# S5 input side: the powers of B one f tile ahead of their transposes, in four fixed slots

## The chip, the cores and the metric

The kernel runs on one core of one Trainium2 chip. The metric is the device time of one execution in microseconds. In the profile PE is TensorE (PEld its weight loads), DVE is VectorE, ACT is ScalarE, POOL is GpSimd, and SP is the engine whose queue issues most of the DMA loads.

## The reference

Two layers act on x of 256 positions by 2048 channels: gated linear attention first, then S5, a complex-diagonal state-space layer. Each has a residual and a layer norm. Of the S5 layer (inner width 4096 = 256 groups of 16 channels, 64 complex states a group) this is the part that matters here:

```
u, z = split(u_in @ w_in)                      # 2 x 4096 columns
lb   = exp(a * dt)                             # lambda, a group's 64 states
bb   = coef * b                                # 64 x 16 a group
x[t] = lb * x[t-1] + bb @ u[t]                 # complex, per group
y[t] = Re(c @ x[t]) + d * u[t]
y    = gelu(y); y = y * sigmoid(y @ w_glu + b_glu); out = (y * silu(z)) @ w_out
```

The kernel does the recurrence in chunks of 8 positions. For that it needs B multiplied by the powers 0 to 7 of lambda (the states' input over a chunk, and the kernel inside a chunk), and a scan over 32 chunks.

## The kernel before, in words

All large products are made from fp32 weights split into a high part (an ACT cast, `hi...`, line 145) and a low part (a DVE subtraction, `lo...`, line 146), and three matmuls on these parts stand for one product. A step of the weight loop is called a block here: one 128 x 1024 piece of weights, its split, and 24 matmuls of 128x128 by 128x256 (lines 180 to 182).

The stage around the change makes u ("su"): eight column groups g = 0 to 7, each of eight blocks kp = 0 to 7. Behind each block, the loop takes steps from a list `bq` as `b_pace` allows (`bstep`), and small steps from another list (`pump`), among them from the end of g = 4 on the 30 scan steps of the first half (`scan`, lines 1187 to 1189). The list `bq` goes through the 256 groups in 32 tiles f of 8 groups, two tiles f = 2p and 2p + 1 to a pair p = 0 to 15:

- `bload(p)` loads B and the powers of lambda of a pair (tile `rb`, two buffers, lines 1056 and 1058, issued on the SP queue), `kload` loads C (`rc`, line 1066).
- `b_pow(f)` makes B times the powers: an ACT copy (line 1091) for power 0 and three DVE instructions of 128x896 for powers 1 to 7 (two products, lines 1096 and 1097, the second into the tile `pt` with one buffer; a subtraction, line 1098). The result is half of the pair's tile `wu[p]`, which the trace calls wb.
- `b_tr(f)` transposes it: twice four PE transposes into a PSUM bank (line 1107, pswb), each four followed by an ACT copy (line 1108) into half of the pair's tile `wb[p]`, which the trace calls wbt.
- `s_mm(p)` multiplies u by it, and C by the powers: 128 small matmuls (lines 1128 and 1133), then two DVE transposes into the states sx (line 1139) and two ACT copies (line 1141).
- `k_out(p)` transposes the chunk's kernel (line 1149), copies it (1152), adds d on POOL (1155, 1158) and stores it with two DMAs of the POOL queue (1161) to dk.

At the end of each g, `s_in(g)` copies the four PSUM banks to the tile vv (ACT, line 1114), stores it (du, line 1115) and loads it back in another order into half of `Ut[g // 2]` (line 1116), both on the POOL queue. s_mm(p) reads `Ut[p // 4]`.

The tiles u1 (four), Ut (four), wu and wb share one pool, `s8`, of twelve slots. Before the change each pair makes a new wu and a new wb tile.

The program's order is not the order on the engines: the tile framework hands out the slots and orders each engine's instructions ahead of time, by its own estimate of when each can start; among those that can start, the one that stands first in the program goes first. On the chip each engine then runs its own list in order.

The last blocks of bq run under g = 0 of the next stage ("sz", the z half of w_in). The steps of bq before the change, in order: f = 0, f = 1; then for each p from 1: s_mm(p - 1), f = 2p, f = 2p + 1, and from p = 2 on k_out(p - 2). With `b_pace` the two first steps run behind kp = 3 and kp = 7 of g = 0, and from kp = 4 of g = 1 on one step runs behind each block.

Of the kernel before, what the change touches and what calls it, by code (L numbers as in the profile page):

```python
# [15 lines left out]
P = 128  # L16
# [17 lines left out]
def trunk(ctx, tc, x, c, ln_g, ln_b, ada_w, ada_b, gla_w_in, gla_gate_w2, gla_gate_b, gla_norm_g,  # L34
# [3 lines left out]
    V, S, PE = nc.vector, nc.scalar, nc.tensor  # L38
# [35 lines left out]
    def s8t(name, shape, dt=F32):  # L74
        return s8.tile([P] + shape, dt, tag="s8", name=name)
# [4 lines left out]
    def psx(name):  # L80
        return ax.tile([P, 512], F32, tag="ax", name=name)

    ident = cp.tile([P, P], F32, name="ident")
# [50 lines left out]
    def wload(src, k0, c0, name, last=False):  # L134
        w = wp.tile([P, 1024], F32, tag="w", name="w" + name) if last else ring.take("w" + name)
        dma(w.rearrange("p (k c) -> p k c", k=2),
            src[k0 * P:(k0 + 2) * P, c0:c0 + 512].rearrange("(k p) c -> p k c", p=P))
        return w
# [3 lines left out]
    def split(w, name):  # L142
        hi = his.take("hi" + name)
        lo = los.take("lo" + name)
        S.copy(hi, w)  # L145
        last_lo[0] = V.tensor_tensor(lo, w, hi.bitcast(F32), op=ALU.subtract).ins  # L146
        return hi.rearrange("p (k c) -> p k c", k=2), lo.rearrange("p (k c) -> p k c", k=2)
# [75 lines left out]
    ps = psx("psc")  # L223
# [225 lines left out]
    ps = psx("psv2")  # L449
# [395 lines left out]
    for h in range(4):  # L845
        ps = psx(f"psst{h}")
        for cc, (r, a, b) in enumerate(((0, 0, 256), (64, 64, 256), (0, 256, 384), (64, 320, 384))):
            for t in range(2):
                PE.matmul(ps[r:r + 64, a:b], lhsT=kt[:, 2 * h + t, cc * 64:cc * 64 + 64], rhs=qs[cc][:, 2 * h + t, :],
                          start=(t == 0), stop=(t == 1))  # L850
# [62 lines left out]
    for g in range(8):  # L913
# [3 lines left out]
        for kp in range(8):  # L917
            for _ in range(-(-len(hq) // (8 * (2 - g % 2) - kp))):
                hq.pop(0)()
            w = split(wload(win, 2 * kp, 6144 + g * 512, f"z{g}{kp}"), f"z{g}{kp}")  # L920
            st_step(banks, u0, w, kp, 15)
            pump(Z_RATE)
        for f in range(4):
            i = (g * 4 + f) % 8
# [103 lines left out]
    for k in range(16):  # L1028
        ps = psx(f"psn{k}")
# [18 lines left out]
    def Uv(f):  # L1048
        return Ut[f // 8][:, (f % 8) // 4, :, f % 4, :]
# [3 lines left out]
    def bload(f2):  # L1053

        a = tp.tile([P, 2, 384], F32, tag="rb", name=f"rb{f2}", bufs=2)
        dma(a[:, :, 0:256], rec[:, 2 * f2:2 * f2 + 2, 128:384])
        for h in range(2):
            dma(a[64 * h:64 * h + 64, :, 256:384], rec[64 - 64 * h:128 - 64 * h, 2 * f2:2 * f2 + 2, 256:384])
        rb[f2] = a
# [3 lines left out]
    def kload(f2):  # L1063

        a = rc[f2] = tp.tile([P, 2, 144], F32, tag="rc", name=f"rc{f2}", bufs=2)
        dma(a, rec[:, 2 * f2:2 * f2 + 2, 0:144])

    wb = {}

    def powmul(o, t, a0, a1, l):  # L1070

        n = o.shape[2]
        bc = lambda z: z.rearrange("p (g i) -> p g i", g=8).unsqueeze(2).to_broadcast([P, 8, n, 16])
        lv = l.rearrange("p (r g n) -> p r g n", r=2, g=8)
        lq = lambda r: lv[:, r, :, :n].unsqueeze(3).to_broadcast([P, 8, n, 16])
        V.tensor_tensor(o, bc(a0), lq(0), op=ALU.mult)
        V.tensor_tensor(t, bc(a1), lq(1), op=ALU.mult)

    wu, kts, Upair = {}, {}, {}

    def b_pow(f):
        p = f // 2
        if f % 2 == 0:

            if p < 15:
                bload(p + 1)

            wu[p] = s8t(f"wb{p}", [2, 8, 16, 8])
        a = rb[p][:, f % 2]
        w = wu[p][:, f % 2]  # L1090
        S.copy(w[:, :, :, 0], a[:, 128:256].rearrange("p (g i) -> p g i", g=8))
        t_ = tp.tile([P, 8, 16, 7], F32, tag="pt", name=f"pt{f}", bufs=1)
        bc = lambda z: z.rearrange("p (g i) -> p g i", g=8).unsqueeze(3).to_broadcast([P, 8, 16, 7])
        lv = a[:, 0:128].rearrange("p (r g n) -> p r g n", r=2, g=8)
        lq = lambda r: lv[:, r, :, :7].unsqueeze(2).to_broadcast([P, 8, 16, 7])
        V.tensor_tensor(w[:, :, :, 1:8], bc(a[:, 128:256]), lq(0), op=ALU.mult)
        V.tensor_tensor(t_, bc(a[:, 256:384]), lq(1), op=ALU.mult)
        V.tensor_tensor(w[:, :, :, 1:8], w[:, :, :, 1:8], t_, op=ALU.subtract)

    def b_tr(f):  # L1100
        p = f // 2
        if f % 2 == 0:
            wb[p] = s8t(f"wbt{p}", [2, 8, 128])
        for h in range(2):
            ps = psx(f"pswb{f}{h}")
            for g in range(4):
                PE.transpose(ps[:, g * P:(g + 1) * P], wu[p][:, f % 2, 4 * h + g].rearrange("p i s -> p (i s)"), ident)
            S.copy(wb[p][:, f % 2, 4 * h:4 * h + 4, :], ps.rearrange("p (g r) -> p g r", g=4))

    def s_in(g, banks):  # L1110

# [7 lines left out]
    def s_mm(p):  # L1119
        pss = [psx(f"pss{2 * p + i}") for i in range(2)]  # L1120
        for i in range(2):
            f = 2 * p + i
            U = Uv(f)
            cc = rc[p][:, i]

            for b in range(2):
                for q in range(4):
                    PE.matmul(pss[i][32 * q:32 * q + 32, b * P:(b + 1) * P], lhsT=U[:, 2 * q + b],
                              rhs=wb[p][:, i, 2 * q + b, :], start=True, stop=True)
            for b in range(2):  # L1130
                for q in range(4):
                    g = 2 * q + b
                    PE.matmul(pss[i][32 * q:32 * q + 32, T + b * P:T + (b + 1) * P], lhsT=cc[:, g * 16:g * 16 + 32],
                              rhs=wu[p][:, i, g].rearrange("p i n -> p (i n)"), start=True, stop=True)
        kt_ = tp.tile([P, 2, 2, P], F32, tag="kt", name=f"kT{p}", bufs=1)
        for i in range(2):
            f = 2 * p + i
            n = 2 * (f % 16)
            V.transpose(sx[:, f // 16, 1:33, :, n:n + 2].rearrange("p c r b -> p b r c"),
                        pss[i][:, :T].rearrange("p (b r l) -> p b r l", b=2, r=4))  # L1140
            S.copy(kt_[:, i].rearrange("p b (n i) -> p b n i", n=8), pss[i][:, T:].rearrange("p (b i n) -> p b n i", b=2, i=16))
        kts[p] = kt_

    def k_out(p):
        kt_ = kts[p]
        pk_ = psx(f"psk{p}")
        for i in range(2):
            for b in range(2):
                PE.transpose(pk_[:, (2 * i + b) * P:(2 * i + b + 1) * P], kt_[:, i, b], ident)
        ks = tp.tile([P, 2, P], F32, tag="ks", name=f"ks{p}", bufs=1)  # L1150
        for i in range(2):
            S.copy(ks[:, i].rearrange("p (q b i) -> p q b i", q=4, b=2),
                   pk_[:, i * T:(i + 1) * T].rearrange("p (b q i) -> p q b i", b=2, q=4)[:, :, :, :16])
        dm = tp.tile([16, 16, 16], F32, tag="dm", name=f"dm{p}", bufs=1)
        nc.gpsimd.tensor_tensor(dm, ident[:16, :16].unsqueeze(1).to_broadcast([16, 16, 16]),
                                dT[:, 16 * p:16 * p + 16].unsqueeze(2).to_broadcast([16, 16, 16]), op=ALU.mult)
        kv = ks[:16].rearrange("p f c -> p (f c)")
        nc.gpsimd.tensor_tensor(kv, kv, dm.rearrange("p g i -> p (g i)"), op=ALU.add)
        for i in range(2):
            f = 2 * p + i  # L1160
            wdma(dk[16 * f:16 * f + 16, 896:1920].rearrange("i (n c) -> n i c", n=8), ks[:, i])


    bq = []
    for p in range(18):
        if 1 <= p < 17:
            bq.append(lambda p=p: s_mm(p - 1))
        for f in (2 * p, 2 * p + 1):
            if f < 32:
                bq.append(lambda f=f: (kload(f // 2) if f % 2 else None, b_pow(f), b_tr(f)))  # L1170
        if p >= 2:
            bq.append(lambda p=p: k_out(p - 2))

    bload(0)
    b_pace = [0.0]
# [15 lines left out]
    for g in range(8):  # L1191
        banks = [psm(f"su{g}{f}") for f in range(4)]
        for kp in range(8):

            with tc.issue_after(normed1) if (g, kp) == (0, 2) else nullcontext():
                w = split(wload(sw, 2 * kp, g * 512, f"su{g}{kp}"), f"su{g}{kp}")
            st_step(banks, u1, w, kp, 15)

            if (g, kp) == (0, 3):
                mid = more(1, 1)  # L1200
            if (g, kp) == (1, 0):
                b_pace[0] = -4.0
            b_pace[0] += 1.0 if g else 0.25
            n = max(0, int(b_pace[0]))
            bstep(n)
            b_pace[0] -= n
            pump(SCAN_RATE)
        s_in(g, banks)
        if g == 4:
            bg.extend([lambda cidx=cidx: scan(cidx, 0) for cidx in range(1, 31)])  # L1210
# [61 lines left out]
    for g in range(8):  # L1272
        banks = [psm(f"sz{g}{f}") for f in range(4)]
        for kp in range(8):
            w = split(wload(sw, 2 * kp, E + g * 512, f"sz{g}{kp}"), f"sz{g}{kp}")
# [4 lines left out]
        for f in range(4):  # L1280
            i = (g * 4 + f) % 8
# [42 lines left out]
    for g in range(8):  # L1324
        banks = [psm(f"gl{g}{f}") for f in range(4)]
        for kp in range(16):
            w = split(wload(s5_w_glu[0], 2 * kp, g * 512, f"gl{g}{kp}"), f"gl{g}{kp}")
# [14 lines left out]
        for f in range(4):  # L1342
            i = g * 4 + f
# [78 lines left out]
    ps = psx("psnb")  # L1422
# [33 lines left out]
```

## Time and profile before

| | |
|---|---|
| time, median of 3 runs | 1836.67 us (1836.52 to 1839.31) |
| time of the profiled execution | 1838.83 us |
| its span, first to last instruction | 1837.1 us |
| mean granted TensorE clock | 0.991 |
| PE busy in the span | 1781.8 us, 97% |
| DVE busy | 1410.3 us, 77% |
| ACT busy | 895.4 us, 49% |
| POOL busy | 88.0 us, 5% |
| HBM read | 437.01 MB |

The stage su lies at about 762 to 1019 us of the span. In the rows of the profile, times are microseconds from the span's start. A row of the timeline has the start, the duration, the engine, the line of the kernel, the operation, what it writes from what it reads, the number of instructions merged, and in brackets the idle time before it and what ended that. A row of the windows has for each engine its busy time and, in brackets, the number of instructions, then the granted clock of PE, the DMA engines' busy share and GB/s.

### The profile page before, as it was taken

To read this page: it belongs to the slowest core of one execution; us is meant where nothing else is said; L and a number is where in the kernel's file an instruction comes from. 1 tells how busy PE (TensorE), PEld (TensorE's weight loads), DVE (VectorE), ACT (ScalarE), POOL (GpSimd) and SP (SyncE) were. 2 spreads that over 40 slices of the span, in tenths; PEclk is the share of its full clock that TensorE was granted. 3 is DMA by queue.
4 is the path that set the end of the run, shared out by engine and by line. 5 is a ranking of instruction groups with operands and counts; after the bars stand their busy time and mean duration, and the time that the engine had idled before them with its cause. 6 is when DMAs were issued, how large, how long until landed. Compare 5 with 4: busy or idle time off the path is not lost.

```text
span 1837.1 us, 33664 instructions
## 1 busy us (share of the span) xinstructions
PE 1781.8 (97%) x13491; PEld 1574.5 (86%) x13491; DVE 1410.3 (77%) x1880; ACT 895.4 (49%) x1266; POOL 88.0 (5%) x94
## 2 busy tenths in 40 slices
PE   7999999999999999999999999999999999999997
PEld 5776897899999888899998999988888888888886
DVE  4887757879999988687699689888577775557556
ACT  4433557556556333654554535545445444444332
POOL 0000000000000000002233300000000000000000
PEclk9999999999999999999999999999999999999998
DMA  9997975879889998486665577999688886668653
GB/s 343 387 342 247 294 247 162 284 258 325 290 289 321 335 356 289 160 264 204 194 202 168 170 213 217 234 246 233 218 278 269 275 271 208 187 192 324 194 185 92
DMA packets 246101, 457.86 MB, mean 249 GB/s; under 512 B 19828, under 2 KB 49198, under 8 KB 244662
## 3 DMA queue, kind: packets, MB, share of 16 engines
q1 hardware_dynamic: 239320, 436.02, 74.1%
q0 software_dynamic: 5856, 18.63, 3.1%
q8 instruction: 106, 1.74, 0.4%
q10 hardware_dynamic: 768, 1.05, 0.2%
q14 instruction: 51, 0.42, 0.1%
HBM read 437.01 MB, written 18.61 MB: 248 GB/s over the span
## 4 chain that ended last, share of the span: by engine, by line
PE 78%; DVE 11%; DMA 4%; issue 3%; ACT 2%; POOL 0%; SPq 0%; DVEq 0%; ACTq 0%; POOLq 0%
PE gl L192 13%; PE gl L193 7%; PE op L168 6%; PE op L169 6%; PE op L167 6%; PE z L182 3%; PE z L181 3%; PE z L180 3%; PE v L168 3%; PE v L169 2%; PE v L167 2%; PE su L180 2%; PE su L181 2%; PE su L182 2%; PE sz L180 2%
## 5 line engine op out<-in xcount | busy, mean ns | idle before, releaser
L146 DVE TENSOR_TENSOR logl<-wgl,higl 128x1024 fp32r<-128x1024 f32 x128 | 156.7, 1224 | 116.0 <-ACT higl L145 111.2
L145 ACT CAST higl<-wgl 128x1024 fp32r<-128x1024 f32 x128 | 134.4, 1051 | 172.4 <-PE gl L192 167.5
L192 PE MATMUL gl<-yp,higl 128*128 128x512 f32 x512 | 179.4, 395 | 0.1
L192 PE MATMUL gl<-yb,higl 128*128 128x512 f32 x512 | 179.1, 395 | 0.0
L145 ACT CAST hio<-wo 128x1024 fp32r<-128x1024 f32 x95 | 100.2, 1055 | 152.8 <-PE op L169 131.9
L146 DVE TENSOR_TENSOR loo<-wo,hio 128x1024 fp32r<-128x1024 f32 x95 | 116.5, 1228 | 66.8 <-ACT hio L145 64.8
L317 DVE SCALAR_TENSOR_TENSOR acc<-wa,cs,acc 128x512 f32<-128x512 f32 x217 | 162.7, 750 | 2.9 <-DMA wa<-in_ada_w 0.2
L180 PE MATMUL sz<-u1h,hisz 128*128 128x256 f32 x512 | 150.4, 294 | 2.3 <-ACT zs L1284 2.3
L180 PE MATMUL su<-u1h,hisu 128*128 128x256 f32 x512 | 151.3, 297 | 0.0
L180 PE MATMUL z<-u0h,hiz 128*128 128x256 f32 x512 | 148.7, 290 | 0.0
L182 PE MATMUL sz<-u1h,losz 128*128 128x256 f32 x512 | 144.5, 283 | 2.1 <-DVE losz L146 2.1
L182 PE MATMUL su<-u1h,losu 128*128 128x256 f32 x512 | 145.8, 285 | 0.0
L181 PE MATMUL su<-u1l,hisu 128*128 128x256 f32 x512 | 145.6, 284 | 0.0
L182 PE MATMUL z<-u0h,loz 128*128 128x256 f32 x512 | 144.9, 283 | 0.6 <-DVE loz L146 0.6
L181 PE MATMUL z<-u0l,hiz 128*128 128x256 f32 x512 | 144.7, 283 | 0.0
L181 PE MATMUL sz<-u1l,hisz 128*128 128x256 f32 x512 | 144.7, 283 | 0.0
L193 PE MATMUL gl<-yb,logl 128*128 128x256 f32 x512 | 143.0, 279 | 0.0
L193 PE MATMUL gl<-yp,logl 128*128 128x256 f32 x512 | 142.3, 279 | 0.0
L145 ACT CAST hisz<-wsz 128x1024 fp32r<-128x1024 f32 x64 | 67.0, 1049 | 113.6 <-PE sz L181 57.4
L192 PEld LDWEIGHTS gl<-yp,higl 128*128 128x128 f32 x512 | 95.9, 188 | 22.9 <-issue 0.6
L192 PEld LDWEIGHTS gl<-yb,higl 128*128 128x128 f32 x512 | 96.0, 188 | 22.6
L145 ACT CAST hiz<-wz 128x1024 fp32r<-128x1024 f32 x64 | 67.2, 1051 | 88.2 <-PE z L181 80.8
(322 smaller groups left out, 5000.8 us busy)
## 6 DMA issues: line engine op xcount, KB each, us to landing
wgl<-in_s_w_glu SPq DMA_DIRECT2D x128, 512.0 KB, 4.8
wa<-in_ada_w SPq DMA_DIRECT2D x116, 512.0 KB, 5.2
wv<-in_gla_w_in SPq DMA_DIRECT2D x64, 512.0 KB, 6.5
wz<-in_gla_w_in SPq DMA_DIRECT2D x64, 512.0 KB, 5.4
wsu<-in_s_w_in SPq DMA_DIRECT2D x64, 512.0 KB, 4.5
wsz<-in_s_w_in SPq DMA_DIRECT2D x64, 512.0 KB, 5.7
wo<-in_s_w_out SPq DMA_DIRECT2D x64, 512.0 KB, 4.7
a<-in_ada_w SPq DMA_DIRECT2D x31, 1024.0 KB, 10.7
```

Source lines behind the costliest of these rows:

```text
L145: S.copy(hi, w)
L146: last_lo[0] = V.tensor_tensor(lo, w, hi.bitcast(F32), op=ALU.subtract).ins
L167: PE.matmul(banks[tt], lhsT=uh, rhs=hi[:, kk, :], start=(k == first), stop=False)
L168: PE.matmul(banks[tt], lhsT=uh, rhs=lo[:, kk, :], start=False, stop=False)
L169: last_mm[0] = PE.matmul(banks[tt], lhsT=ul, rhs=hi[:, kk, :], start=False, stop=(k == last)).ins
L180: PE.matmul(o, lhsT=wh, rhs=u.hi(k), start=(k == first), stop=False)
L181: PE.matmul(o, lhsT=wh, rhs=u.lo(k), start=False, stop=False)
L182: last_mm[0] = PE.matmul(o, lhsT=wl, rhs=u.hi(k), start=False, stop=(k == last)).ins
L192: PE.matmul(banks[f], lhsT=hi[:, kk, fs], rhs=u.both(k), start=(k == 0), stop=False)
L193: PE.matmul(banks[f][:, :T], lhsT=lo[:, kk, fs], rhs=u.hi(k), start=False, stop=(k == last))
L317: V.scalar_tensor_tensor(acc[0], w[:, kk, :], cs[:, k:k + 1], acc[0], op0=ALU.mult, op1=ALU.add)
```

## The change

`wu` and `wb` become four tiles that are made once, two of each, and used in turn by pairs (index p % 2). `b_pow(f + 1)` now stands ahead of `b_tr(f)` in the step of f, with `b_pow(0)` as a first step of its own; `bload(p + 1)`, which `b_pow(2p)` issues, moves with it. The counter at the start of g = 1 is set to -3 instead of -4, so that the longer list still has s_mm(0) behind kp = 4 of g = 1. The places of s_mm, k_out and b_tr from there on stay.

```diff
-    wu, kts, Upair = {}, {}, {}
+    kts = {}
+    wu = [s8t(f"wu{i}", [2, 8, 16, 8]) for i in range(2)]
+    wb = [s8t(f"wbt{i}", [2, 8, 128]) for i in range(2)]

     def b_pow(f):
         p = f // 2
         if f % 2 == 0:
             if p < 15:
                 bload(p + 1)
-            wu[p] = s8t(f"wb{p}", [2, 8, 16, 8])
         a = rb[p][:, f % 2]
-        w = wu[p][:, f % 2]
+        w = wu[p % 2][:, f % 2]
...
     def b_tr(f):
         p = f // 2
-        if f % 2 == 0:
-            wb[p] = s8t(f"wbt{p}", [2, 8, 128])
...
-                PE.transpose(ps[:, g * P:(g + 1) * P], wu[p][:, f % 2, 4 * h + g].rearrange("p i s -> p (i s)"), ident)
-            S.copy(wb[p][:, f % 2, 4 * h:4 * h + 4, :], ps.rearrange("p (g r) -> p g r", g=4))
+                PE.transpose(ps[:, g * P:(g + 1) * P], wu[p % 2][:, f % 2, 4 * h + g].rearrange("p i s -> p (i s)"), ident)
+            S.copy(wb[p % 2][:, f % 2, 4 * h:4 * h + 4, :], ps.rearrange("p (g r) -> p g r", g=4))
...
-    bq = []
+    bq = [lambda: b_pow(0)]
     for p in range(18):
         if 1 <= p < 17:
             bq.append(lambda p=p: s_mm(p - 1))
         for f in (2 * p, 2 * p + 1):
             if f < 32:
-                bq.append(lambda f=f: (kload(f // 2) if f % 2 else None, b_pow(f), b_tr(f)))
+                bq.append(lambda f=f: (kload(f // 2) if f % 2 else None, b_pow(f + 1) if f < 31 else None, b_tr(f)))
         if p >= 2:
             bq.append(lambda p=p: k_out(p - 2))
...
             if (g, kp) == (1, 0):
-                b_pace[0] = -4.0
+                b_pace[0] = -3.0
```

In s_mm the two reads of wb[p] and wu[p] become wb[p % 2] and wu[p % 2].

More of the change, by code (lines that the diff above doesn't have):

```diff
@@ L1066, in kload @@
         dma(a, rec[:, 2 * f2:2 * f2 + 2, 0:144])
-    wb = {}
     def powmul(o, t, a0, a1, l):
@@ L1128, in s_mm @@
                     PE.matmul(pss[i][32 * q:32 * q + 32, b * P:(b + 1) * P], lhsT=U[:, 2 * q + b],
-                              rhs=wb[p][:, i, 2 * q + b, :], start=True, stop=True)
+                              rhs=wb[p % 2][:, i, 2 * q + b, :], start=True, stop=True)
             for b in range(2):
@@ L1133, in s_mm @@
                     PE.matmul(pss[i][32 * q:32 * q + 32, T + b * P:T + (b + 1) * P], lhsT=cc[:, g * 16:g * 16 + 32],
-                              rhs=wu[p][:, i, g].rearrange("p i n -> p (i n)"), start=True, stop=True)
+                              rhs=wu[p % 2][:, i, g].rearrange("p i n -> p (i n)"), start=True, stop=True)
         kt_ = tp.tile([P, 2, 2, P], F32, tag="kt", name=f"kT{p}", bufs=1)
```

## The prediction

> **What bounds the kernel now.** I read the page's span and engine shares, then the waits of the one stage that the diff touches, then that stage window by window, and last the order of each engine's instructions around its holes.
>
> ```profile
> span 1837.1 us, 33664 instructions
> PE 1781.8 (97%) x13491; PEld 1574.5 (86%) x13491; DVE 1410.3 (77%) x1880; ACT 895.4 (49%) x1266; POOL 88.0 (5%) x94
> PE pswb L1107 <- DVE wb L1098: 4.7, 3, 3.1
> ```
>
> TensorE (PE) sets the time: busy for 97%, so only what closes its holes counts. The last row is PE's longest wait between 760 and 1060 us (engine, line, releaser: total, times, longest), and the one that the change can touch: transposes of B (L1107) waited three times, 4.7 us in all, for VectorE (DVE) to finish the powers (L1098).
>
> ```profile
> core 0: us, PE busy (x) PEld busy (x) DVE busy (x) ACT busy (x) POOL busy (x), PEclk, DMA share, GB/s
> 783.00:790.00 7.00, 6.05 (x52) 5.87 (x51) 6.86 (x7) 2.66 (x6) 0.00 (x0) 1.00 0.84 268
> 901.00:917.00 16.00, 16.00 (x184) 15.27 (x179) 5.92 (x6) 7.98 (x16) 3.61 (x5) 1.00 0.55 157
> 910.00:930.00 20.00, 19.32 (x204) 18.10 (x204) 14.98 (x23) 10.87 (x23) 5.28 (x6) 1.00 0.58 169
> 923.00:985.00 62.00, 60.81 (x687) 57.68 (x687) 61.35 (x105) 32.62 (x63) 25.73 (x20) 1.00 0.65 193
> 990.00:1000.00 10.00, 7.40 (x49) 7.26 (x50) 10.00 (x17) 4.33 (x7) 0.95 (x1) 0.83 0.58 162
> 787.35 1.06 PE L1107 MATMUL pswb<-ident,wb 128*128 128x128 f32 x8 [0.95 <-DVE wb L1098]
> 992.60 1.09 PE L1107 MATMUL pswb<-ident,wb 128*128 128x128 f32 x4 [3.06 <-DVE wb L1098]
> 966.20 0.65 PE L1128 MATMUL pss<-wbt,U 128*32 128x128 f32 x16 [0.51 <-DMA U<-du]
> ```
>
> The three holes are 7.00 - 6.05 = 0.95 at 787, 20.00 - 19.32 = 0.68 near 923, and 3.06 before 992.60. After the last one the granted clock is 0.83 over 10 us: (1 - 0.83) x 10 = 1.7 us lost on top. DVE is full in the rows from 923 on (61.35 of 62) and has 16.00 - 5.92 = 10.1 us free from 901 to 917.
>
> **Why the last two.** The twelve slots of one pool hold u1 (4), Ut (4) and the pairs' tiles wu (traced as wb) and wbt. A new tile takes its slot at its first write, and first writes stand in program order. A pair's powers begin with a ScalarE (ACT) copy (L1091):
>
> ```profile
> 873.54 0.58 ACT L1108 COPY wbt<-pswb 128x512 f32<-128x512 f32 x1
> 874.02 0.68 ACT L1091 COPY wb<-rb 128x128 f32<-128x128 f32 x2
> 917.13 0.37 ACT L1114 COPY vv<-su 128x256 f32<-128x256 f32 x1
> 917.39 0.68 ACT L1091 COPY wb<-rb 128x128 f32<-128x128 f32 x2
> 983.30 0.37 ACT L1114 COPY vv<-su 128x256 f32<-128x256 f32 x1
> 983.57 0.67 ACT L1091 COPY wb<-rb 128x128 f32<-128x128 f32 x2
> ```
>
> Normally (874.02) it stands right behind the first wbt copy of the pair before, so powers are a pair ahead already. But the copies of f = 16 and 24 stand behind the vv copies (L1114) that close g = 4 and 6. There s_in first writes Ut[2] and Ut[3], of the same pool; that this is the blocker I infer from the match. The rest of f = 24 shows it too:
>
> ```profile
> 971.92 1.08 DVE L1097 TENSOR_TENSOR pt<-rb 128x896 f32<-128x896 f32 x1
> 990.16 1.09 DVE L1096 TENSOR_TENSOR wb<-rb 128x896 f32<-128x896 f32 x1
> 991.37 1.09 DVE L1098 TENSOR_TENSOR wb<-wb,pt 128x896 f32<-128x896 f32 x1
> ```
>
> Its second product (L1097), which needs no s8 slot, ran at 971.92; the first, which writes wu, only at 990.16. In between DVE did scans and low halves; the scans are read only by the x transposes of the next stage (L1241).
>
> **The change part by part.**
> *Fixed slots.* wu and wbt take their slots once, and Ut[1] to Ut[3] no longer stand in the way. Powers then wait only for the s_mm two pairs back, whose last matmuls are
>
> ```profile
> 901.32 0.62 PE L1133 MATMUL pss<-wb,rc 128*32 128x128 f32 x16
> 967.51 0.65 PE L1133 MATMUL pss<-wb,rc 128*32 128x128 f32 x16
> ```
>
> for f = 16 (s_mm(6), read by 902) and f = 24 (s_mm(10), by 968.2). The first find DVE's 10.1 free us: one tile costs three products of 1.09, 3.3 us, so both tiles of the pair (6.6) fit. The second come among the scans, some 20 us before they are needed. The holes of 0.68 and 3.06 close, and with the latter the 1.7 us of half clock: 5.4 us. Bounds: 0 (the holes stay) to 5.4. I take all of it, since the steady pairs, with the same work and DVE as full, show none: PE's idle time from 923 to 985, 62.00 - 60.81 = 1.2, is the 0.68 and the 0.51 for a U load.
>
> *One tile ahead.* It moves three DVE products and one ACT copy one block earlier in program order for odd f, three for even f (past k_out(p - 3) and s_mm(p - 1)); with the even ones go three load issues (L1056, L1058), past three weight issues on the SP queue. On POOL nothing moves, but k_out's and s_in's instructions there now compete with other DVE work (a rival below). The loads wait for the powers of the tile before, which move too, so SP waits as it did: 0. If a load came late, its 4.36 us from start to landing (row below) would stand before ACT's copy and the weight casts behind it. On DVE the transposes of s_mm(p - 1) can now stand behind one tile of powers, 3.3 us, while PE wants their bank a block (2.9, row below) later: 0.4 a pair, 2.0 for the five pairs of the full stretch as the bad end; I take 0, since where powers run early they are done by then. Instruction counts do not change.
>
> *Start.* b_pow(0) keeps its place (fourth block of g = 0), the transposes of f = 0 and 1 and the powers of f = 2 move four, four and two blocks; b_pace goes from -4 to -3 so that s_mm(0) stays in the fifth block of g = 1.
>
> ```profile
> 778.60 4.36 DMA rb<-rec
> 786.12 0.28 PE L182 MATMUL su<-u1h,losu 128*128 128x256 f32 x1
> 788.17 0.36 PE L180 MATMUL su<-u1h,hisu 128*128 128x256 f32 x1
> 791.91 0.36 PE L180 MATMUL su<-u1h,hisu 128*128 128x256 f32 x1
> 788.01 1.08 ACT L1108 COPY wbt<-pswb 128x512 f32<-128x512 f32 x2 [4.34 <-PE pswb L1107]
> 788.97 1.06 ACT L145 CAST hisu<-wsu 128x1024 fp32r<-128x1024 f32 x1
> 790.50 2.35 DVE L146 TENSOR_TENSOR losu<-wsu,hisu 128x1024 fp32r<-128x1024 f32 x2
> ```
>
> At 786.12 seven blocks are done; PE waits, transposes, runs the eighth from 788.17 to 791.1, transposes f = 1 and starts g = 1 at 791.91, when the low half from 790.50 is just there. Afterwards the eighth block can run at 786.3 and end at 789.2, the first transposes (0.8) at 790.0; then PE waits for that low half. If the cast at 788.97 still stands behind the transposes' copies, copies, cast and subtraction (1.08 + 1.06 + 1.2) end at 793.3: 1.4 later than now, with the second transposes (0.8) still to do: +2.2. If it moves ahead of them, PE gains the hole: -1.0. Since the next work is late in its turn, I take 0.
>
> **Sum.** 0.68 + 3.06 + 1.7 = 5.4. The profiled execution took 1838.83 (span 1837.1): 1833.4. It lies 2.2 above the median of the runs, 1836.67, so I predict 1831.2. A difference under 0.2% (3.7 us) can't be told from none.
>
> **A rule beside the row.** Another hole bears on the 1.7:
>
> ```profile
> 1214.51 0.66 PE L1256 MATMUL psy<-mt,U 128*32 128x128 f32 x8 [2.10 <-DMA mt<-dk]
> 1214.00:1218.00 4.00, 3.49 (x52) 3.14 (x53) 0.81 (x1) 2.49 (x3) 0.00 (x0) 0.57 0.98 238
> 1066.00:1072.00 6.00, 3.94 (x33) 3.74 (x32) 6.00 (x10) 1.97 (x3) 0.00 (x0) 1.00 0.86 211
> 1072.00:1076.00 4.00, 4.00 (x36) 4.00 (x35) 3.90 (x9) 0.00 (x0) 0.00 (x0) 1.00 1.02 306
> ```
>
> A hole of 2.10 at 1214 was followed by a clock of 0.57 over 4 us, one of 2.06 (6.00 - 3.94) before 1072 by full clock. So a hole of two or three microseconds may or may not cost 1.7 more, and with all later work shifted such a charge can come or go: +-1.7 on the range. The Trainium skill (TensorE: Matmul & The Clock Gate, Part 1: The HAM clock gate) says that the clock falls to half after an idle window of about 3.4 us, and that the windows run freely. By the length alone our 3.06 would not suffice, and the sum would be 3.7 instead of 5.4; the trace, with a charge after 2.10, disagrees with the length.
>
> **The rivals.**
> *The half clock is not the hole's* (as that length would have it): 3.06 and 0.68 close, 1.7 stays: 1832.9. Against: the half-clock stretch starts within the hole's end. 0.10.
>
> *DVE is the bound.* Its 61.35 of 62 leaves no room; the planner keeps scans (earlier in the program) ahead and the 3.06 and 1.7 stay or move to the low halves: 0.7 gained, 1836.0. For: DVE's fullness. Against: 6.6 us of powers leave that stretch for 901 to 917. 0.15.
>
> *The start gets worse.* The late cast above makes a hole of 3.3 (790.0 to 793.3), and a half clock of 1.7 with it; less the 0.95 that goes: +4.1, so 1835.3. 0.10.
>
> *POOL is held up.*
>
> ```profile
> 948.19 4.79 POOL L1158 TENSOR_TENSOR ks<-ks,dm 16x256 f32<-16x256 f32 x1 [10.27 <-ACT ks L1152]
> 981.10 0.74 POOL L1158 TENSOR_TENSOR ks<-ks,dm 16x256 f32<-16x256 f32 x1 [9.26 <-ACT ks L1152]
> 990.47 0.95 POOL L1116 DMA_DIRECT2D U<-du  x1 [5.63 <-DVE sca L1187]
> 1029.18 4.69 DMA U<-du
> 1003.18 0.57 PE pss L1128 x16
> ```
>
> The add of k_out took 4.79 where DVE ran powers, 0.74 at 981 where it ran scans. With powers there it may take 4.1 longer, and s_in's two DMAs stand behind it: U lands at 990.47 + 4.69 + 4.1 = 999.3, while s_mm(12) would start at 1003.18 - 5.4 = 997.8. A new wait of 1.5: 1832.7. The Trainium skill (SBUF — State Buffer, Who interferes with whom) says that a DVE instruction with two SBUF inputs contends with a GpSimd one that reads SBUF; the trace agrees at 948 and less so at 981. 0.07.
>
> *Slower: the fixed slot makes DVE wait for PE.* Powers of f = 2p overwrite what s_mm(p - 2) reads. If they stand at the head of DVE's queue before PE is there, the low halves behind them wait as well:
>
> ```profile
> DVE losu L146 <- PE pss L1133: 4.3, 2, 2.1
> ```
>
> 2.1 us each. In the full stretch there are five pairs: 10.5 lost on DVE, which PE must wait out, against 5.4 gained: 1841.8. It turns slower beyond the bound from 9.1 / 2.1, more than four such waits. Against: DVE's transposes of s_mm already stand there and wait for the same matmuls. 0.08.
>
> **Numbers.** The forecast has the other 0.50; its own range is 1829.5 to 1833.0. Low end 1828.8: the start gains 1.0 and a half clock goes elsewhere (1.4 of 1.7). High end 1837.0: the DVE case with 1 us of the start's loss. Left out are the slower case and the tails of the rest. Faster than 1833.0: the forecast and most of the two cases just below the bound, 0.58; slower 0.09; within 0.33.
>
> **What would show it.** Copies L1091 of f = 16 and 24 near 902 and 968, no longer behind L1114; powers of f = 16 in DVE's idle time at 901 to 917; no wait of L1107 for L1098 beyond the start; clock 1.00 between 985 and 1000; scans between 973 and 990 thinned out by powers. Wrong, if L1091 still lags at every eighth f, if the hole reappears before L1128 or losu, or if the stages behind have other holes than now.

## The result, and the profile after

The changed kernel took 1828.49 us (median of 4 runs, 1825.60 to 1830.32) beside 1837.99 of the kernel before (4 runs, 1836.52 to 1839.43): a ratio of 0.9949, interval 0.9934 to 0.9964. Two later comparisons gave 0.9959 (0.9943 to 0.9974) and 0.9958 (0.9943 to 0.9974). So the gain is 7.4 to 9.5 us where 5.4 was forecast, and the first median lies 0.3 us under the range. The profiled execution took 1828.37, 10.5 less than the one before. Single runs of the kernel before went from 1830.17 to 1842.49 in 33 runs.

First the page's head, then the same windows as in the prediction, both of the changed kernel:

```profile
span 1826.6 us, 33659 instructions
PE 1780.4 (97%) x13491; PEld 1573.1 (86%) x13491; DVE 1411.3 (77%) x1880; ACT 898.9 (49%) x1266; POOL 86.3 (5%) x94
```

```profile
783.00:790.00 7.00, 7.00 (x61) 7.00 (x60) 6.90 (x7) 4.00 (x8) 0.00 (x0) 1.00 0.85 261
901.00:917.00 16.00, 15.36 (x175) 14.79 (x176) 11.99 (x12) 7.63 (x15) 1.92 (x2) 1.00 0.55 166
910.00:930.00 20.00, 20.00 (x214) 19.07 (x213) 15.11 (x21) 11.31 (x21) 5.28 (x6) 1.00 0.67 202
923.00:985.00 62.00, 61.77 (x698) 58.81 (x697) 61.28 (x106) 34.12 (x64) 17.38 (x16) 1.00 0.65 193
990.00:1000.00 10.00, 10.00 (x115) 9.66 (x117) 10.00 (x17) 5.64 (x10) 3.31 (x2) 1.00 0.68 228
```

PE's work is the same (1780.4 against 1781.8 us); the span is shorter because holes are gone. All three holes before the transposes are closed, and the clock from 990 to 1000 is 1.00 instead of 0.83. DVE's busy time from 901 to 917 (the third figure of that row behind the width) rose from 5.92 to 11.99 us: the powers of two tiles moved there. One new hole stands in the second row, 16.00 - 15.36 = 0.64 of it within the window.

The order on ACT and DVE around the places where the copies used to lag (L1089 was L1091, L1110 was L1114, L1094 to L1096 were L1096 to L1098; the trace now calls the tile wu):

```profile
902.78 0.44 ACT L1089 COPY wu<-rb 128x128 f32<-128x128 f32 x1 [2.05 <-PE pss L1129]
903.65 0.47 ACT L1089 COPY wu<-rb 128x128 f32<-128x128 f32 x1 [0.43 <-PE pss L1129]
917.20 0.37 ACT L1110 COPY vv<-su 128x256 f32<-128x256 f32 x1 [0.23 <-PE su L182]
967.73 0.44 ACT L1089 COPY wu<-rb 128x128 f32<-128x128 f32 x1
```

```profile
904.16 2.06 DVE L1094 TENSOR_TENSOR wu<-rb 128x896 f32<-128x896 f32 x2
906.14 1.08 DVE L1096 TENSOR_TENSOR wu<-wu,pt 128x896 f32<-128x896 f32 x1
```

The copies of f = 16 stand at 902.78 and those of f = 24 at 967.73 (902 and 968 were forecast), ahead of the vv copies and right behind the s_mm that frees the slot. Two groups of waits of the su stage, and in the timeline the holes behind the second:

```profile
DVE losu L146 <- PE pss L1129: 12.9, 6, 2.2
PE pss L1124 <- DMA U<-du: 2.6, 3, 1.9
```

```profile
806.36 0.65 PE L1124 MATMUL pss<-wbt,U 128*32 128x128 f32 x16 [0.49 <-DMA U<-du]
901.64 0.64 PE L1124 MATMUL pss<-wbt,U 128*32 128x128 f32 x16 [1.92 <-DMA U<-du]
```

What PE waits for in s_mm is now the load of U: 2.6 us, 1.92 of it at 901.64.

Where the time went shows best when three profiles of either kernel are set against each other. The times of four PE instructions, as differences to the first profile of before (1056.23, 1084.28, 1288.97, 1830.32):

| PE's first matmul of | before, three profiles | after, three profiles | difference of the means | gained since the row above |
|---|---|---|---|---|
| group 1 of the z stage | 0, +0.36, -0.07 | -5.46, -4.05, -6.55 | -5.45 | -5.45 |
| group 2 of the z stage | 0, +1.88, +0.34 | -7.09, -5.59, -8.13 | -7.68 | -2.23 |
| the GLU stage | 0, -4.20, -0.97 | -11.31, -9.10, -11.43 | -8.89 | -1.21 |
| the last one of all | 0, -3.69, -0.25 | -10.44, -9.78, -10.77 | -9.02 | -0.13 |

The stage that the prediction worked out gave 5.45, as forecast. Another 2.2 in the mean, and 1.5 or more in every pair of profiles, came in a stretch of 28 us right behind it. A further 1.2 came behind that, where the profiles of one kernel differ by up to 6 us among themselves.

### The profile page after: what moved, and what is told of

The parts are those of the page before. It is cut to its first block, busy times and chain, and to the rows that moved or that the text cites. A ratio compares the mean times of both kernels' runs of the same rounds, so it can differ in the third digit from the quotient of the medians.

```text
span 1826.6 us, 33659 instructions
## 1 busy us (share of the span) xinstructions
PE 1780.4 (97%) x13491; PEld 1573.1 (86%) x13491; DVE 1411.3 (77%) x1880; ACT 898.9 (49%) x1266; POOL 86.3 (5%) x94
## 4 chain that ended last, share of the span: by engine, by line
PE 83%; DVE 6%; DMA 5%; ACT 3%; issue 3%; SPq 1%; POOL 0%; DVEq 0%; ACTq 0%; POOLq 0%
PE gl L192 13%; PE gl L193 7%; PE op L168 6%; PE op L169 6%; PE op L167 6%; PE v L168 3%; PE z L182 3%; PE z L181 3%; PE z L180 3%; PE v L169 3%; PE v L167 3%; PE sz L180 3%; PE sz L182 2%; PE su L180 2%; PE sz L181 2%
```

## The experiments

**Which half of the change, and was it the U tiles?** Three kernels split it.

The fixed slots alone:

```diff
 after:
-    bq = [lambda: b_pow(0)]
+    bq = []
-    ... b_pow(f + 1) if f < 31 else None, b_tr(f) ...
+    ... b_pow(f), b_tr(f) ...
-                b_pace[0] = -3.0
+                b_pace[0] = -4.0
```

> The four fixed slots alone: the list of steps and the pace are those of the kernel before. Theory A (the U tiles, taking a slot at their first write, held up the powers of every eighth f; any change that lifts this is worth the same): powers of f = 16 run in 901 to 917, the holes before the transposes near 923 and 992 and the half clock behind the latter are gone, the stage ends 5.0 to 5.6 us earlier, and the whole lies within 2 us of the changed kernel (1827 to 1830). Rival B (the order, one tile ahead, makes the gain): the 3.06 hole stays, 1835 to 1838. For the stage behind (1050 to 1290), theory C (it follows: the last store of ks frees the space of the first scan of the second half, and VectorE is full behind it): 4 to 6 us more there. Rival D (the holes there come and go by themselves between executions): the gain there is not tied to the 5.4, 0 to 6 us.

Measured: 1826.39 us (10 runs), ratio 0.9948 (0.9930 to 0.9966). The su holes at 923 and 992 are gone and the clock stays at 1.00; the z stage's group 1 begins 5.52 us earlier than in the first profile of before, as in the changed kernel. The hole at 787 stays (1.06). So the slots alone have the whole gain, and none is seen that the new order adds; the median lies 0.6 us under the expected range.

One tile ahead alone:

```diff
 before:
-    bq = []
+    bq = [lambda: b_pow(0)]
-    ... b_pow(f), b_tr(f) ...
+    ... b_pow(f + 1) if f < 31 else None, b_tr(f) ...
-                b_pace[0] = -4.0
+                b_pace[0] = -3.0
```

> One tile ahead alone: new order and pace, but each pair makes new tiles wu and wb as before. Theory A: with powers one step earlier in the program, those of f = 8, 16, 24 come ahead of the U tile's first write, so the block is lifted here too: 1827 to 1831, with the holes at 923 and 992 gone. Rival B2 (only the fixed slots lift the block): 1835 to 1838, hole of about 3 us before the transposes of f = 24. The 0.95 hole at 787 goes, as in the changed kernel, by the earlier b_pow(0); it is replaced by one of about 0.5 at 806.

The kernel before, U tiles claimed early:

```diff
 before:
     Ut = [s8t(f"U{i}", [2, 8, 4, 32]) for i in range(4)]
+    for i in range(1, 4):
+        V.memset(Ut[i][:, 0, 0, 0, 0:1], 0.0)
```

> The kernel before, and three one-element memsets of Ut[1], Ut[2], Ut[3] on VectorE ahead of the stage, so that these take their slots at once. Nothing else changes. Theory A: this alone closes the holes at 923 and 992 (3.7 us) and ends the half clock (1.7): 5.4 us by the end of the stage, 1827 to 1832. Rival E (the U tiles are not what held the copies; VectorE's fullness or the buffers of wu and wb were): 1835 to 1838 and the copies of f = 16 and 24 still behind the vv copies. The 0.95 hole at 787 stays.

Measured: 1830.60 (0.9979, 0.9962 to 0.9996) and 1830.77 (0.9972, 0.9959 to 0.9985). The first is the kernel one tile ahead, the second the one with the memsets. In both the three late copies of before (852.54, 917.39 and 983.57, for f = 8, 16 and 24) are gone and every pair's powers come in the same place, ahead of the vv copies. Three one-element memsets do that, so the U tiles' late claim was the blocker. That was inferred before, now it is shown. But by the ratios both gain only 4 to 5 us, the slots 9.5. One reason is this, in the kernel with the memsets: the timeline of POOL and the end of a wait on PE (L1160, L1118 and L1130 are the add, the U load and s_mm there), then two windows.

```profile
980.25 5.83 POOL L1160 TENSOR_TENSOR ks<-ks,dm 16x256 f32<-16x256 f32 x1 [8.45 <-ACT ks L1154]
986.37 1.23 POOL L1163 DMA_DIRECT2D dk<-ks  x2 [0.29 <-POOL ks L1160]
988.18 0.62 POOL L1117 DMA_DIRECT2D du<-vv  x1
993.07 0.95 POOL L1118 DMA_DIRECT2D U<-du  x1 [4.27 <-DMA du<-vv]
999.93 0.76 PE L1130 MATMUL pss<-wbt,U 128*32 128x128 f32 x16 [2.19 <-DMA U<-du]
```

```profile
985.00:1000.00 15.00, 12.81 (x109) 12.24 (x112) 14.79 (x29) 7.79 (x14) 8.02 (x7) 1.00 0.74 229
1000.00:1010.00 10.00, 10.00 (x118) 9.41 (x119) 8.53 (x13) 2.69 (x5) 4.82 (x4) 0.83 0.62 179
```

The add of k_out took 5.83 us where before, beside scans, it took 0.74; s_in's two DMAs stand behind it, U is issued 2.6 us later than before, and s_mm(12) waits 2.19 with a half clock behind it (0.83 over 10 us). The kernel one tile ahead shows the same, 2.17 and 0.83. This is the prediction's rival of the POOL queue, in its place; its price there was a wait of 1.5, here it is 2.19 and a half clock.

**Is it the add?**

```diff
 before, U tiles claimed early:
-        dm = tp.tile(...)
-        nc.gpsimd.tensor_tensor(dm, ..., op=ALU.mult)
-        kv = ks[:16].rearrange("p f c -> p (f c)")
-        nc.gpsimd.tensor_tensor(kv, kv, dm..., op=ALU.add)
```

> The kernel with the U tiles claimed early, and both POOL instructions of k_out left out (dm and the add), so that d is missing in the chunk's kernel. Theory P (the hole of 2.19 us before s_mm at 1000 and the half clock behind it come from POOL: the add took 5.83 us beside VectorE's products and held up s_in's two DMAs): U is issued 3 to 5 us earlier than 993.07, the hole and the half clock go, 3.9 us less than with the adds: about 1826 to 1828. Rival Q (the chain from the vv copies over du to U is too long by itself, the add not in it): hole and clock stay, 1829 to 1832.

Measured: 1829.02 (4 runs), ratio 0.9950 (0.9936 to 0.9964), against 0.9972 with the adds. Timeline and a window:

```profile
982.50 0.60 POOL L1117 DMA_DIRECT2D du<-vv  x1 [1.73 <-ACT vv L1116]
987.58 0.92 POOL L1118 DMA_DIRECT2D U<-du  x1 [4.48 <-DMA du<-vv]
997.03 0.65 PE L1130 MATMUL pss<-wbt,U 128*32 128x128 f32 x16
```

```profile
1000.00:1010.00 10.00, 10.00 (x84) 9.60 (x83) 9.96 (x14) 4.92 (x9) 0.00 (x0) 1.00 0.64 187
```

U is issued at 987.58 instead of 993.07, the hole and the half clock are gone: theory P. With a half clock of 1.7 the add had cost 3.9 us at this place. The total is 1 us above the expected range, and the two intervals touch; the rows decide here. In the changed kernel the add was as slow (5.17 at 981, 6.45 at 997). It escaped because its transfers were shorter: du landed 3.2 us after its issue and U 4.8, against 4.6 and 6.7 with the memsets (5.5 and 7.1 one tile ahead), so that U was there 1.9 us before s_mm(12) read it at 998.90. Why they were shorter is not shown.

**Can the waits for U be removed as well?** Here every s_mm comes one block later.

```diff
 after:
-                b_pace[0] = -3.0
+                b_pace[0] = -4.0
```

> The changed kernel with the counter at g = 1 set to -4 instead of -3: every s_mm runs one block (4.04 us) later against the U load that it reads. Theory U (what the changed kernel still loses in the su stage are waits of s_mm for the U load, 0.49 + 1.92 us in one profile of it and 1.78 + 0.91 + 0.38 in the other): all holes at L1124 between 800 and 1030 go, 2.4 to 3.1 us; total 1825.5 to 1827 if the end of the list, now one step later in the next stage, costs nothing. Rival G (given back: k_out of the last pair is a block later, so the scans of the second half start up to 4 us later and VectorE, full behind them, makes PE wait 1 to 3 us more near 1065 and 1110): 1827.5 to 1831.

Measured: 1828.61 (5 runs), ratio 0.9948 (0.9934 to 0.9961), the same as the changed kernel within the intervals. Both theories held in their part. In the su stage no wait for U is left and the z stage begins 9.17 us earlier than before (5.8 at most in the changed kernel). Then it is given back (timeline, then a window):

```profile
1055.95 0.43 DVE L1183 TENSOR_TENSOR sca<-sx,l 128x256 f32<-128x256 f32 x1 [2.06 <-DMA dk<-ks]
1066.35 0.39 PE L182 MATMUL sz<-u1h,losz 128*128 128x256 f32 x1 [3.35 <-DVE losz L146]
```

```profile
1060.00:1120.00 60.00, 55.12 (x613) 52.55 (x613) 57.44 (x106) 28.17 (x40) 0.00 (x0) 0.97 0.78 226
```

**Why did 2.2 us more come behind the stage?** In these 28 us the instructions stand in the same order on PE, ACT, DVE and POOL before and after. But the first scan of the second half (L1187 before, L1183 after) waits for a transfer. Rows of the timeline of before, then of after:

```profile
1052.88 1.22 POOL L1161 DMA_DIRECT2D dk<-ks  x2 [0.29 <-POOL ks L1158]
1057.45 0.43 ACT L1152 COPY ks<-psk 128x128 f32<-128x128 f32 x2 [1.70 <-DMA dk<-ks]
1059.03 1.22 POOL L1161 DMA_DIRECT2D dk<-ks  x2 [0.30 <-POOL ks L1158]
1062.13 0.43 DVE L1187 TENSOR_TENSOR sca<-sx,l 128x256 f32<-128x256 f32 x1 [6.82 <-DMA dk<-ks]
1071.43 0.39 PE L182 MATMUL sz<-u1h,losz 128*128 128x256 f32 x1 [2.06 <-DVE losz L146]
```

```profile
1047.43 1.22 POOL L1157 DMA_DIRECT2D dk<-ks  x2 [0.29 <-POOL ks L1154]
1050.49 0.43 ACT L1148 COPY ks<-psk 128x128 f32<-128x128 f32 x2 [0.20 <-DMA dk<-ks]
1052.07 1.22 POOL L1157 DMA_DIRECT2D dk<-ks  x2 [0.29 <-POOL ks L1154]
1055.05 0.43 DVE L1183 TENSOR_TENSOR sca<-sx,l 128x256 f32<-128x256 f32 x1 [5.20 <-DMA dk<-ks]
1064.34 0.39 PE L182 MATMUL sz<-u1h,losz 128*128 128x256 f32 x1 [1.08 <-DVE losz L146]
```

The scan is the first write to a new pool of tiles (tmp2), and waits until the last of the old pool (tmp1) is done, the store of ks of p = 15. That tile has one buffer, so the last ks copy in turn waits for the store of p = 14, which took 4.6 us from issue to copy before and 3.1 after. The zs evacuations stand behind that copy on ACT, and PE waited for one of them near 1058 (0.40, 0.23 and 0.81 in the three profiles of before, no hole after). From the scan on DVE is full (18.8 to 19.7 of each 20 us from 1070 to 1130, before and after), and the low halves of the z stage queue behind: the later the scans begin against PE, the longer PE waits near 1065 to 1071. The scan came 5.90, 5.76 and 6.33 us behind PE's first matmul of group 1 in the three profiles of before, 4.28, 4.37 and 4.35 in those of after. Two experiments move that point. The one above (-4.0) made it later by leaving a step more for the z stage; this one by four more adds and subtractions of POOL that cancel:

```diff
 after, in k_out:
         nc.gpsimd.tensor_tensor(kv, kv, dm..., op=ALU.add)
+        if p == 15:
+            for op in (ALU.subtract, ALU.add, ALU.subtract, ALU.add):
+                nc.gpsimd.tensor_tensor(kv, kv, dm..., op=op)
```

> The changed kernel with four more POOL adds and subtractions of dm in the last k_out (p = 15), which cancel and take about 3 us, so that the last store of ks comes 3 us later. Nothing else is changed; a planner that knows of them may put a low half ahead of a scan. Theory C (the first scan of the second half waits for the last store of all of the pool tmp1, and VectorE is full from there to about 1150): the first scan starts 3 us later against the stage, and the holes near 1065 and 1108, 2.1 us in both profiles of the changed kernel, grow to 4 to 5 us. Rival H (VectorE has room, these holes have other causes): they stay within 0.5 us of 2.1.

Measured: 1831.35 in one run. The planner also put a low half ahead of a scan and moved some instructions behind it on DVE and PE, so the kernel differs in more than the delay. Timeline and a window:

```profile
1058.13 0.42 DVE L1186 TENSOR_TENSOR sca<-sx,l 128x256 f32<-128x256 f32 x1 [2.34 <-DMA dk<-ks]
1067.06 0.58 PE L182 MATMUL sz<-u1h,losz 128*128 128x256 f32 x1 [3.75 <-DVE losz L146]
```

```profile
1060.00:1120.00 60.00, 55.74 (x613) 53.57 (x613) 56.68 (x102) 23.93 (x36) 0.00 (x0) 0.94 0.77 222
```

With the other kernels, by how late the scan is (its start behind PE's first matmul of group 1; the two main holes of PE from 1060 to 1120, of which only the first lies between groups 1 and 2; what PE lost, or gained with a minus, from group 1 to group 2 against the first profile of before):

| kernel | scan behind group 1 | holes | clock | from group 1 to 2 |
|---|---|---|---|---|
| after, -4.0 | 8.28 | 3.35 + 1.31 | 0.97 | +2.24 |
| after, late store | 7.67 | 3.75 + 0.51 | 0.94 | +3.70 |
| before, three profiles | 5.76 to 6.33 | 2.06 + 1.68, 2.26 + 0.35, 2.06 + 1.83 | 1.00, 0.97, 1.00 | 0, +1.52, +0.41 |
| before, U tiles claimed early | 5.84 | 2.07 + 0.81 | 0.97 | +1.43 |
| after, slots alone | 4.80 | 1.59 + 1.28 | 1.00 | -1.12 |
| before, one tile ahead | 4.52 | 1.32 + 0.89 | 1.00 | -1.40 |
| after, three profiles | 4.28 to 4.37 | 1.08 + 1.00, 1.16 + 0.87, 1.14 + 1.52 | 1.00 | -1.63, -1.54, -1.58 |

Theory C holds for the first hole: it is 1.1 to 1.6 us where the scan comes up to 4.8 us behind group 1, 2.1 to 2.3 near 6 us, and 3.4 to 3.8 near 8. The second, mostly a wait for zs on ACT, does not follow the lateness. In the kernel with the late store 3.3 us later cost 5.3 us in this stretch, holes and half clock together. The mean of the last column in the two rows with three profiles differs by the 2.2 us: 1.0 by the first hole, 0.5 by the hole near 1058 and 0.6 by the half clock that one of three profiles of before has here.

Why the store of p = 14 took 1.5 us less after the change stands in the trace's records of DMA packets. Up to the store's landing ACT, DVE and POOL work at the same times against group 1 in both kernels. But before the change two loads of instructions (8 and 16 KB, over queues of their own) start among the store's packets. Rows of the DMA view (queue, kind: packets, MB, share of the 16 engines), before from 1054.0 to 1055.2, after from 1048.5 to 1049.7, both from 2.2 to 1.1 us ahead of group 1:

```profile
q0 software_dynamic: 83, 0.12, 36.6%
q8 instruction: 1, 0.02, 6.5%
q14 instruction: 1, 0.01, 3.6%
```

```profile
q0 software_dynamic: 87, 0.12, 37.1%
```

In each of the three profiles of before, the last two 4 KB packets of the store start only behind the 16 KB load, the first of them within 0.02 us of its end, and the second of the store's two DMAs lands 3.7 to 4.3 us after its issue. In each of the three of after that load starts when all packets are through, and the DMA lands after 2.3 to 2.4. With the U tiles claimed early the load holds the store up again (3.5), and the scan is late. So most of the 2.2 us came by way of a transfer and not of the powers: the store no longer met a load of instructions. By the three profiles of each kernel that belongs to the program and not to the execution. What sets the time of the load no run shows, and none moved it by itself.

**And what came behind 1150?** One more profile of the changed kernel, and two of the kernel before:

> The changed kernel once more, for a second profile. Theory C (the gain between 1050 and 1290 is caused by what went before): the same holes as in the first profile within 0.3 us each (1.1 near 1064, 1.0 near 1108, 1.0 near 1206, 1.15 near 1250, no half clock there). Rival D (it is chance): holes there differ by 1 us and more from the first profile, and a half clock may appear.

> The kernel before once more, for a second profile. Theory C or any cause in the program for what lies behind 1150: the holes before L1256 at 1214, 1257 and 1280 (5.1 us) and the half clock at 1214 (1.7 us) are there again, within 1 us in sum. Rival D (they come and go between executions with the DMA traffic): another sum, between 1.3 and 5 us, or no half clock at that place, as the five profiles of other versions show 1.3 to 5.5 us there. The holes of the su stage (0.95, 0.68, 0.51, 3.06, 1.20) are there again by both.

> The kernel before, third profile. What belongs to the program comes again: the holes 0.9, 0.7, 3.1 to 3.6 and 0.8 to 1.2 of the su stage with a half clock behind 992; the first scan of the second half 5.7 to 6.0 us behind the second group of the next stage (4.3 to 4.4 in three profiles of the changed kernel); a hole of 2.0 to 2.3 near 1071. By chance (rival D), anything between the two profiles so far (1.2 and 5.1 us of holes and with or without 1.7 of half clock) behind 1195; if it belongs to the program, one of these two sums within 0.5.

Measured: 1828.76 (12 runs, 0.9959) for the first, 1835.11 and 1838.82 us in one run each for the others. The window from 1195 to 1295, of before in its first, second and third profile:

```profile
1195.00:1295.00 100.00, 94.83 (x1315) 87.99 (x1314) 85.82 (x102) 56.15 (x91) 0.00 (x0) 0.98 0.95 238
```

```profile
1195.00:1295.00 100.00, 98.20 (x1342) 90.93 (x1342) 89.73 (x108) 59.43 (x94) 0.00 (x0) 1.00 0.98 253
```

```profile
1195.00:1295.00 100.00, 95.12 (x1324) 88.05 (x1323) 86.87 (x104) 57.53 (x92) 0.00 (x0) 1.00 0.97 244
```

And of after in its first and second:

```profile
1195.00:1295.00 100.00, 97.60 (x1284) 89.61 (x1283) 85.13 (x100) 58.53 (x91) 0.00 (x0) 1.00 0.93 250
```

```profile
1195.00:1295.00 100.00, 96.03 (x1277) 88.44 (x1276) 84.63 (x100) 58.12 (x91) 0.00 (x0) 1.00 0.95 246
```

The DMA engines are 93 to 98% busy. PE's holes are 5.2, 1.8 and 4.9 us before, all before L1256, which waits for mt, and 2.4, 4.0 and 3.7 in the three profiles after, before the same line (now L1252), most of them for mt; 2% of the clock is gone in one profile only. They come and go with the execution: rival D. So the first profile of before had bad luck here, the half clock above all, and a part of the 10.5 between the two first profiles is no gain at all. The su holes, by contrast, came again (0.93, 0.68, 3.64 and 0.81 in the second profile; 1.11, 0.68, 0.22, 3.64 and 1.09 in the third).

**A faster version?** The end of the list was moved forward, with and without the later s_mm.

```diff
 after, with -4.0 (first kernel) or -3.0 (second), z stage, g = 0:
-                bstep(1 + kp % 2)
+                bstep(1 + (kp > 0))
```

> The changed kernel with the counter at -4 (s_mm a block later) and, under g = 0 of the next stage, two steps of the list behind each block from the second on instead of one and two in turn. The last k_out then runs two blocks earlier than with -4 alone, one earlier than in the changed kernel. Theory C with U: the su stage ends 9 us earlier than before (the U waits gone, as with -4 alone), and the first scan of the second half starts about 8 us (two blocks) earlier against the stage than with -4 alone, so that the 3.36 hole and the half clock behind it go: holes near 1065 and 1112 together under 2 us, total 1822 to 1826, the best of all versions. Rival K (PE and ACT have more list steps in each block, s_mm of the last pairs waits for U or for the powers instead): 2 to 4 us of new holes between 1015 and 1050, total 1826 to 1830.

> The changed kernel with the faster end of the list alone (the counter at -3): the last k_out one block earlier than in the changed kernel. Theory C: the first scan of the second half starts about 4 us earlier against the stage (4.3 us behind its second group in both profiles, then 0 to 1), the holes near 1065 and 1108 (2.1 in sum) fall under 1 us, and the total by 1 to 2 us against the changed kernel: 1826 to 1828. Rival K: s_mm of the last pairs waits for U, 1 to 3 us, and nothing is gained: 1828 to 1830.

> The changed kernel beside the two versions above, for the comparison on one chip and a third profile: 1827 to 1830 by theory C and by rival K alike. U waits between 800 and 1030 of 1 to 3 us in sum (2.4 and 3.1 in the profiles so far), 2.0 to 2.2 us near 1065 and 1108; behind 1150 any sum from 0.5 to 5 us by rival D, 2.5 to 4 if that part belongs to the program.

Measured on one chip, in the order of these three: 1826.67 (6 runs; 0.9945, 0.9927 to 0.9962), 1828.24 (11 runs; 0.9962, 0.9947 to 0.9976) and the changed kernel 1828.67 (6 runs; 0.9958, 0.9943 to 0.9974). The first has the lowest median of the three, but the intervals overlap: not told apart. It lies 0.7 us above the expected range, and the mechanism held in part only: the scan came 6.51 us behind group 1, only 1.8 and not 8 earlier than with -4.0 alone, and holes of 2.07 and 2.51 stayed. ACT's rows tell why:

```profile
1047.43 1.28 ACT L1280 ACT_TABLE_LOAD   x1
1048.73 0.38 ACT L1280 ACTIVATE zs<-sz 128x256 f32<-128x256 f32 x1
1050.87 0.43 ACT L1148 COPY ks<-psk 128x128 f32<-128x128 f32 x2 [1.75 <-DMA dk<-ks]
1051.18 0.96 ACT L1280 ACTIVATE zs<-sz 128x256 f32<-128x256 f32 x3
```

The last ks copy again waits for the one ks buffer, now in the midst of the zs evacuations, which PE waits for as well. In the second kernel the scan came 2.39 us behind group 1, but the holes did not fall under 1 us as expected (0.82, 0.78 and 1.24, where the changed kernel has 2.0 to 2.7 in sum). So theory C holds for a late scan, and one earlier than in the changed kernel gained nothing here. That DVE has the same work to do either way is the likely reason; it isn't shown.

## Why the prediction was right or wrong

- **The blocker and the sum of the stage: right.** The holes of 0.68 and 3.06 and the half clock went, for 5.4 forecast and 5.45 measured over three profiles each. That the number fits so well is partly luck, errors that cancel. In the means of three profiles the three terms were 0.68, 3.45 and 2.27, in all 6.4 us (the second profile of before lost 3.4 to the half clock). The start gave 0.4 more. The waits of s_mm, nearly all for U, which the sum left as they were, took 0.8 (1.7, 0.8 and 1.3 us before; 2.6, 3.2 and 0.5 after), and a half clock near 760, ahead of the change, took 0.6.
- **Start and "one tile ahead" at 0: near enough as a sum.** The 0.95 at 787 went and others took its place, near 791 and, waiting for U, near 806; at the third group of the su stage PE stood at -0.12, +1.99 and +0.40 against the first profile of before. No gain of the order is seen: with the slots alone it is the same.
- **The rest of the kernel at 0: the step that failed.** The sum ended with the su stage and took everything behind it as unchanged, but for +-1.7 of a half clock. The runs show 2.2 us there, which puts the forecast of 1831.2 at 1829.0. The path was in the profile of before: DVE waits 6.82 us for the store of ks, and PE then 2.06 for DVE. That this path could move was there to be read, and the prediction itself named other holes behind the stage as a sign of being wrong. That it moved by 1.5 us, because the store of p = 14 no longer met a load of instructions, was not in the prediction's rows, and it is luck as far as these runs show.
- **The profiled execution against the median.** Setting it down by 2.2 was right in direction: behind 1195 the first profile of before had 5.2 us of holes and a half clock, where another had 1.8. Which part of the 2.2 that is isn't shown.
- **The POOL rival (0.07): wrong here, right next door.** Two kernels with unblocked powers lost 2.2 us and a half clock to it; the changed kernel's s_mm(12) read U without a wait, by 1.9 us. Its reason was too narrow: the add is slow beside any unbroken run of DVE instructions, not beside powers alone (see the end).
- **The slower rival: its count came true and its price did not.** DVE's wait of the low half behind s_mm grew from 4.3 us in 2 waits to 12.9 in 6, so by 8.6 us and about the four waits from which it was to decide. PE lost nothing by it: PE idled 62.00 - 61.77 = 0.23 from 923 to 985. The low halves are finished 5 to 11 us ahead of their use there, and the waits ate only of that.
- **DVE as the bound (0.15) and the half clock that stays (0.10)**: neither; DVE is as full as it was (61.28 of 62) and PE loses nothing by it.

## What to carry to other kernels

A stage's end is not the end of a change: look for the first instruction behind it that waits for something the stage produces last (here a store that frees a pool of tiles), and for the engine that is full from there on. A wait on an engine that works ahead costs nothing until its lead is used up, so read the lead beside the wait. A gain behind the stage need not be the change's own: ask which instruction or transfer first differs, and by how much, before it is counted. And before a difference between two profiles is explained, take a second profile of the kernel before: holes behind a busy DMA can differ by 3 us and a half clock between two executions of one program.

## What the runs showed of the hardware

**The half clock.** After every hole of PE of 3.06 us or more in these stages (993 in three profiles, 1066, 1067) matmuls ran at half speed. Holes of 1.9 to 2.5 us did it at times: the same hole of 2.35 us at 60 us of the span was followed by it in 5 of 14 profiles, holes of 2.07, 2.17, 2.19 and 2.26 were, others of 2.06, 2.07, 2.11 and 2.51 were not. The Trainium skill (TensorE: Matmul & The Clock Gate, Part 1) has a free-running window of 3.4 us. The records of the granted clock agree with the window and show what decides: in each of the 14 profiles the stretches of half clock between 30 and 1800 us start whole multiples of 3.413 us apart and last 3.41 or 6.83 us. All 48 start behind a window of this grid in which PE was busy for at most 0.48 of the time; of the windows below that, three (0.42 to 0.46) had no such stretch behind them. So where a hole lies against the grid matters: the 2.10 us before 1214.51 lay almost wholly in the window that ends at 1214.40 and cost 1.7 us, the 2.06 before 1071.43 were divided by a border at 1071.04 (busy for 0.51 of the window before it) and cost nothing more.

**POOL beside DVE.** The add of 16x256 took 0.7 to 1.6 us in most places and 2.8 to 7.1 us where the instructions of DVE followed one another without a gap: products, low halves and scans alike. In the changed kernel the add of 5.17 us at 981 had 1.3 us of powers beside it, while one of 0.94 us at 1013.80 had powers beside it for nearly all its time, in two instructions with a gap of 0.03 us between them. The Trainium skill (SBUF — State Buffer, Who interferes with whom) says that a DVE instruction with two SBUF inputs contends with a GpSimd one that reads SBUF; the trace agrees, and the run without the adds shows the price on PE, 3.9 us.

**Loads of instructions.** They go over the DMA engines too (queues 8 and 14 of the DMA view). Here one packet of 16 KB, in flight for 1.2 to 1.7 us, held up the last two packets of a store of 64 KB; by the chain above PE then waited 1 us longer some 15 us later.
